# Layer 1 of a two-layer decoder trunk: attention's results and gates stored by token tiles, rows of dilation 16 by halves of the sequence

## The chip, the cores and the metric

The kernel runs on one core of a Trainium2 chip. The metric is the device time of one launch in microseconds (us), the median of several runs. A core has TensorE (PE; its weight loads are listed apart as PEld), VectorE (DVE), ScalarE (ACT), GpSimd (POOL) and SyncE (SP), each with an instruction queue of its own that is worked through in order, and 16 DMA engines that move data between the chip's memory (HBM) and the on-chip memory (SBUF). A DMA is issued by an engine's queue, here SP's (queue 1 in the profile) or GpSimd's (queue 0), and lands some microseconds later.

## The reference, cut to what matters

One inference step of a two-layer trunk, for a prompt of 2048 tokens and 32 sample tokens (8 sequences of 4). D_MODEL is 1024; a layer's width splits into 768 for the mixer and 256 for attention over 256 memory tokens.

```python
def mixer_layer(x, mem_k, mem_v, branch, w_in, w_out, ln_g, ln_b):
    proj = x @ w_in
    u, gate, mq, mgate = jnp.split(proj, IN_SPLITS, axis=-1)
    y, aux = branch(u)
    y = y.astype(x.dtype) * jax.nn.silu(gate)
    m = mem_attention(mq, mem_k, mem_v).astype(x.dtype) * jax.nn.silu(mgate)
    out = jnp.concatenate([y, m], axis=-1) @ w_out
    return layer_norm(DEEPNORM_ALPHA * x + out, ln_g, ln_b), aux
```

Layer 0's branch is a diagonal state-space mixer. Layer 1's is dilated causal attention in three groups of four heads: windows of 128, 512 and 2048 tokens with dilation 1, 4 and 16, all over one shared K and V that are projected from the residual stream after layer 0. The three groups' outputs are weighted by a softmax over the groups' log-sum-exps, and K and V are outputs too.

## The kernel before

Activations stand transposed, features on the 128 partitions and tokens along the free axis; a token tile has 128 tokens, so there are 16 for the prompt and one (number 16) for the sample's 32. An fp32 product is made of three reduced-precision ones: `split` (lines 123 and 124) makes a rounded high part on ScalarE (`ch`, `XH`, `wh`) and the remainder on VectorE (`cl`, `XL`, `wl`), and `mm3` (lines 128 to 130) issues the three matmuls.

Layer 1 is a list of projections (units) on TensorE, between which generators of side work (memory attention, `dilated`, `dil_sample`) issue their own matmuls at a set rate. Each unit ends in an evacuation that stores its result to HBM: `evac_streams` stores rows of q and k to `e_qT` and `e_kT` with the tokens ordered by residue of the dilation (for dilation 16, in 16 runs of 64 tokens a row and half sequence), `evac_gate` (lines 286 to 294) makes SiLU gates with ScalarE and VectorE and stores them to `e_gA` and `e_gB` from SP. Its tile `s` has three buffers.

`mem_attention` stores its result `ct` to `e_cm` (line 972), `dilated` stores `oT`, 128 features x 2048 tokens, to `e_oT` after every four quarters (line 1637, six such stores), and `dil_sample_end` stores the sample's to `e_cs`; these go by GpSimd's queue. `dilated` loads q and k rows into `raw` (lines 1551, 1552) and splits them: ScalarE makes `qh`, VectorE `ql` (line 1005).

The last part is `out_last`. For each of the 17 token tiles (order 0 to 7, 16, 8 to 15) `cat_dilated` loads attention's result into `ot` in two DMAs, 2 feature tiles from `e_cm` (line 1833) and 6 from `e_oT` (1834), the gate (1837) and the groups' weights `fb` (1842), all from SP. GpSimd multiplies `ot` by `fb` (1848), VectorE multiplies it by the gate (1849), ScalarE and VectorE split it into `ch` and `cl`, TensorE does 2 x 8 x 3 matmuls of 512 columns, and VectorE adds the residual `xres` (line 1963), takes statistics (1964) and normalises (1933, 1934); GpSimd issues the store of `y`. `ot`, `gate` and `fb` have four buffers, `xres` three, `ch` and `cl` two. The tile two ahead is multiplied and the next one split before a tile's matmuls, and a tile's loads are asked for five tiles ahead; a load starts when a buffer is free, that is, when the `cl` of the tile four before is done. `first1` makes the first two tiles already during the last gate projections, in the buffers of others (`v`, `wraw`).

The order on each engine is made by a scheduler from the recorded program. SP has one queue for all its loads and stores: an instruction that waits holds all that come behind it.

Of the kernel before, what the change touches and what calls it, by code (L numbers as in the profile page):

```python
# [9 lines left out]
F32 = mybir.dt.float32  # L10
# [3 lines left out]
OP = mybir.AluOpType  # L14
# [4 lines left out]
D = 1024  # L19
# [40 lines left out]
class Trunk:  # L60
# [223 lines left out]
    def evac_gate(self, dst, m):  # L284

        nc = self.nc

        def f(hf, off, n, p):
            s = self.ev.tile([128, 512], F32, name="s", bufs=3)
            nc.scalar.activation(s[:, :n], p[:, :n], AF.Tanh, scale=0.5)  # L290
            nc.vector.scalar_tensor_tensor(s[:, :n], s[:, :n], 1.0, p[:, :n], op0=OP.add, op1=OP.mult)  # L291
            self.recent = s[0:1, 0:1]
            nc.sync.dma_start(dst[hf][m * 128:m * 128 + 128, off:off + n], s[:, :n])
        return f

    def evac_copy(self, dst, m):
        nc = self.nc
# [590 lines left out]
    def mem_attention(self, l, d, side):  # L888
# [3 lines left out]
        with self.pool("ma", side=side) as p, self.pool("maps", space=PSUM, side=side) as psum:  # L892
# [60 lines left out]
            def st3(m):  # L953
                j, t = divmod(m, 2)
                ht, c0 = at(j)
                if t == 0:
                    O[j] = psum.tile([128, 512], F32, name="o", bufs=1)
                o, pt = O[j], PT.pop(m)
                for y in range(2):
                    for k in range(2):  # L960
                        for h in range(2):
                            c = (ht * 2 + h) * 64
                            mm(o[h * 64:h * 64 + 64, (t * 2 + y) * 128:(t * 2 + y) * 128 + 128], V[:, k, c:c + 64],  # L963
                               pt[:, y, h, k], start=k == 0, stop=k == 1)
                if t < 1:
                    return
                ct = p.tile([128, 512], F32, name="ct", bufs=2)
                if l == 0:
                    v.scalar_tensor_tensor(ct, o, 0.5, MG[j], op0=OP.mult, op1=OP.mult)
                else:  # L970
                    self.copy_out(ct, o)
                self.q2.dma_start(d["cm"][ht * 128:ht * 128 + 128, c0:c0 + 512], ct)

            load(0)
            load(1)
# [26 lines left out]
    def split_q(self, qh, ql, raw):  # L1002

        self.nc.scalar.activation(qh, raw, AF.Copy, scale=-0.125)
        self.nc.vector.scalar_tensor_tensor(ql, raw, -0.125, qh.bitcast(F32), op0=OP.mult, op1=OP.subtract)

    def scores(self, s, q, k, ts, ks=slice(None)):

# [8 lines left out]
    def mem_sample(self, l, p, psum, d):  # L1017
# [54 lines left out]
        for c in range(2):  # L1072
            pp = slice(c * 64, c * 64 + 64)
            for ht in range(2):
# [4 lines left out]
                                           op0=OP.mult, op1=OP.mult)  # L1079
                else:  # L1080
                    v.tensor_copy(view(ct[pp], ht * NS, dims), src)
        self.q2.dma_start(d["cm"][:, S:NT].rearrange("(m p) t -> p m t", p=128), ct)

    def softmax_rows(self, p, s, n, name):

# [287 lines left out]
    def layer1_units(self, d):  # L1373
# [3 lines left out]
        def evac_streams(dst, m, outs):  # L1377

            g = m // 2
            dil = DILS[g]  # L1380
            rows = {}

            def f(hf, off, n, p):
                if off == 0:
                    rows[hf] = self.ev.tile([128, HALF], F32, name="row", bufs=2)
                row = rows[hf]
                b = min(n, HALF - off) // 64
                s0 = off // 64
                src = p[:, :b * 64]
                if g == 0:  # L1390
                    out, src = view(row, s0, [[1, b], [16, 64]]), src.rearrange("p (b k) -> p b k", k=64)
                elif g == 1:
                    out = view(row, s0 // 4, [[1, b // 4], [256, 4], [4, 64]])
                    src = src.rearrange("p (a r k) -> p a r k", r=4, k=64)
                else:
                    out = row[:, off:off + b * 64]
                self.copy_out(out, src)
                self.recent = row[0:1, 0:1]
                if n > b * 64:
                    u = self.ev.tile([128, NS], F32, name="us", bufs=2)  # L1400
                    nc.vector.tensor_copy(u, p[:, b * 64:n])
                    nc.sync.dma_start(dst[m * 128:m * 128 + 128, S:NT], u)
                    if outs:
                        nc.sync.dma_start(o["ks"][m * 128:m * 128 + 128, :], u)
                if off + b * 64 < HALF:
                    return
                run = HALF // dil
                to = [[NT, 128], [S // dil, dil], [1, run]]
                nc.sync.dma_start(dview(dst, m * 128 * NT + hf * run, to), row.rearrange("p (r k) -> p r k", r=dil))
                if not outs:  # L1410
                    return
                r = slice(m % 2 * 128, m % 2 * 128 + 128)
                if g == 2:
                    nc.sync.dma_start(o["k2"][r, :, hf * 64:hf * 64 + 64], row.rearrange("p (r k) -> p r k", r=dil))
                elif hf:
                    nc.sync.dma_start(o[f"k{g}"][r], view(row, run - 128, [[run, dil], [1, 128]]))
            return f
# [103 lines left out]
    def dilated(self, p, psum, g, d):  # L1521
# [18 lines left out]
        def load(j):  # L1540

            hp, qd = divmod(j, 4)
            c = g * 2 + hp
            k0 = max(qd * 4 - 1, 0) if g == 0 else qd * 4
            n = (qd * 4 + 4 - k0) * 128
            if qd == 0:
                NB[hp] = p.tile([128, 2, 256], F32, name="NB", bufs=2)
                self.q2.dma_start(NB[hp], i["nbias"][2 * c:2 * c + 2].rearrange("h p u -> p h u"))
            raw = p.tile([128, 512 + W], F32, name="raw", bufs=3)
            rows = slice(c * 128, c * 128 + 128)  # L1550
            self.q2.dma_start(raw[:, 0:512], d["qT"][rows, qd * 512:qd * 512 + 512])
            self.q2.dma_start(raw[:, 512:512 + n], d["kT"][rows, k0 * 128:k0 * 128 + n])
            RAW[j] = raw

        def load_v(j):
# [4 lines left out]
            self.q2.dma_start(V[j][:, 0:n // 128], dview(d["V"], (g * 16 + k0) * 32768 + hp * 128,  # L1560
                                                         [[256, 128], [32768, n // 128], [1, 128]]))

        def prep(j, part):

            qd = j % 4
            k0 = max(qd * 4 - 1, 0) if g == 0 else qd * 4
            n = (qd * 4 + 4 - k0) * 128
            raw = RAW[j]
            if part == 0:
                q = [p.tile([128, 512], F32R, name=nm, bufs=2) for nm in ("qh", "ql")]  # L1570
                self.split_q(*q, raw[:, 0:512])
                QK[j] = q, k0
            else:
                k = [p.tile([128, W], F32R, name=nm, bufs=2) for nm in ("kh", "kl")]
                self.split(k[0][:, 0:n], k[1][:, 0:n], raw[:, 512:512 + n])
                QK[j] = QK[j][0], k, k0

        def st1(m):
# [29 lines left out]
        def st3(m):  # L1608
# [25 lines left out]
                src = o.rearrange("p (s f k) -> p s f k", s=4, f=2)  # L1634
                self.copy_out(view(oT[hp], qd * 256, [[64, 4], [HALF, 2], [1, 64]]), src)
            if qd == 3:
                self.q2.dma_start(d["oT"][c * 128:c * 128 + 128, :], oT[hp])

        load(0)
        load_v(0)  # L1640
# [158 lines left out]
    def dil_sample_end(self, p, psum, d):  # L1799
# [17 lines left out]
        for g in range(3):  # L1817
# [5 lines left out]
                    v.tensor_copy(view(ct[pp], (g * 2 + ht) * NS, [[1, 8], [8, 4]]),  # L1823
                                  view(tp[pp], ht * 64 + c, [[8, 8], [2, 4]]))
            yield
        self.q2.dma_start(d["cs"].rearrange("(m p) t -> p m t", p=128), ct)

    def cat_dilated(self, d, bufs=2):
        nc = self.nc

        def load(p, tt, ts, n):
            ot = p.tile([128, 8, 128], F32, name="ot", bufs=bufs)
            nc.sync.dma_start(ot[:, 6:8, :n], d["cm"][:, ts].rearrange("(k p) t -> p k t", p=128))
            nc.sync.dma_start(ot[:, 0:6, :n], (d["oT"][:, ts] if tt < 16 else d["cs"]).rearrange("(k p) t -> p k t", p=128))
            gt = p.tile([128, 8, 128], F32, name="gate", bufs=bufs)
            h, a = (0, tt * 128) if tt < 8 else (1, tt * 128 - HALF)
            nc.sync.dma_start(gt[:, :, :n], d["g"][h][:, a:a + n].rearrange("(k p) t -> p k t", p=128))
            fb = None
            if tt < 16:
                fb = p.tile([128, 6, 128], F32, name="fb", bufs=bufs)  # L1840
                for h in range(2):
                    nc.sync.dma_start(fb[h * 64:h * 64 + 64], dview(d["f"], (tt * 2 + h) * 768, [[0, 64], [128, 6], [1, 128]]))
            return ot, gt, fb
# [155 lines left out]
def _dram1(pool, d):  # L1999
    def t(name, *shape):  # L2000
        return pool.tile(list(shape), F32, name="e_" + name)

    return {"x1": d["x1"], "x1T": d["x1T"], "qT": t("qT", MIX, NT), "kT": t("kT", MIX, NT), "V": t("V", 3, 16, 128, 256),
            "vs": t("vs", NS, MIX), "g": (t("gA", D, HALF), t("gB", D, XW)), "mq": t("mq", MEMW, NT),
            "mk": d["mk"], "mv": d["mv"], "cm": t("cm", MEMW, NT), "cs": t("cs", MIX, NS), "oT": t("oT", MIX, S), "st": t("st", 3, 2, 4, S),
            "f": t("f", 16, 2, 6, 128)}


OUTS = {"y": (NT, D), "ssm_p": (128, G), "ssm_s": (128, 24, 2, 8), "mem_k": (2, 256, 256), "mem_v": (2, 256, 256),
        "k0": (256, 1, 128), "k1": (256, 4, 128), "k2": (256, 16, 128), "ks": (MIX, NS), "v0": (128, 256), "v1": (4, 128, 256),  # L2010
        "v2": (16, 128, 256), "vs": (NS, MIX), "n_cache_dil1_kv": (8, 124, 512), "n_cache_dil4_kv": (8, 508, 512),
        "n_cache_dil16_kv": (8, 2044, 512)}

# [161 lines left out]
```

## Time and profile before

| | us |
|---|---|
| median of 3 runs (lowest, highest) | 1985.59 (1984.99, 1986.73) |
| the profiled execution | 1987.37 |
| its span, first to last instruction | 1985.6 |
| TensorE busy in the span | 1933.8 (97 %) |
| VectorE busy | 1177.6 (59 %) |
| ScalarE busy | 687.6 (35 %) |
| GpSimd busy | 419.0 (21 %) |
| mean granted clock of TensorE | 0.991 |

All times of rows are counted from the span's start. An engine's idle time is put down to what ended last before the instruction started; a releaser is inferred from events, so two things that end together can be taken for each other. TensorE's matmuls are pipelined: a duration is longer than the distance from one start to the next. The granted clock is 1.00 at 2.4 GHz and 0.50 at 1.2 GHz.

### The profile page before, as it was taken

What the parts mean: (1) busy time and instruction counts of PE and PEld (TensorE: products, weight loads), DVE (VectorE), ACT (ScalarE), POOL (GpSimd) and SP (SyncE); (2) the same over time, 40 slices, a digit from 0 to 9 for tenths busy, and PEclk for the clock granted to TensorE, in tenths of its full rate; (3) what the DMA queues carried; (4) which work ended last, traced back from release to release, by engine and by line L of the source; (5) the groups of instructions that cost most, each with busy time, mean ns of one, the idle gap of its engine ahead of it and who ended that gap; (6) DMA issues with size and microseconds to landing.
All of it is one profiled execution on the core that took longest, in us unless ns stands there. A gap on an engine that the chain in (4) does not pass through costs nothing.

```text
span 1985.6 us, 35812 instructions
## 1 busy us (share of the span) xinstructions
PE 1933.8 (97%) x13446; PEld 1649.3 (83%) x13446; DVE 1177.6 (59%) x2758; ACT 687.6 (35%) x1585; POOL 419.0 (21%) x754
## 2 busy tenths in 40 slices
PE   8999999999989999999999999999999999999998
PEld 6789888888769988787898879898888877888777
DVE  8639989885575756667456336532651246345685
ACT  5333222333453421115445226522661246231110
POOL 0404444313332012220000020003102200412220
PEclk9999999999999999999999999999999999999999
DMA  7685556656367899978533266437648636759951
GB/s 227 173 252 133 163 170 188 203 184 219 111 170 220 238 307 347 362 268 262 165 124 115 90 222 195 135 91 200 192 119 247 223 111 191 256 169 263 285 164 70
DMA packets 410694, 388.44 MB, mean 196 GB/s; under 512 B 99801, under 2 KB 356233, under 8 KB 407241
## 3 DMA queue, kind: packets, MB, share of 16 engines
q1 hardware_dynamic: 384472, 257.52, 44.5%
q0 software_dynamic: 26048, 128.63, 19.0%
q8 instruction: 106, 1.74, 0.4%
q14 instruction: 68, 0.55, 0.1%
HBM read 280.30 MB, written 150.27 MB: 217 GB/s over the span
## 4 chain that ended last, share of the span: by engine, by line
PE 77%; DVE 9%; DMA 8%; issue 2%; POOL 2%; SPq 1%; ACT 1%; DVEq 0%; POOLq 0%; ACTq 0%
PE mm L128 20%; PE mm L129 20%; PE mm L130 20%; PE s L1014 4%; PE o L1620 2%; PE tp L1605 2%; DMA bcraw<-in_ssm_bc 2%; PE o L963 2%; DMA ot<-e_oT 2%; PE tp L950 1%; DMA xraw<-in_xT 1%; DVE wl L124 1%; DVE H L675 1%; PE tp L1366 1%; DMA craw<-d_cm 1%
## 5 line engine op out<-in xcount | busy, mean ns | idle before, releaser
L128 PE MATMUL mm<-XH,wh 128*128 128x512 f32 (+2 forms) x1520 | 546.9, 360 | 13.8 <-ACT wh L123 7.4
L129 PE MATMUL mm<-XH,wl 128*128 128x512 f32 (+2 forms) x1520 | 540.3, 356 | 0.3 <-DVE wl L124 0.3
L130 PE MATMUL mm<-XL,wh 128*128 128x512 f32 (+2 forms) x1520 | 538.2, 355 | 1.5 <-DVE XL L124 1.4
L128 PEld LDWEIGHTS mm<-XH,wh 128*128 128x128 f32 x1520 | 287.5, 189 | 60.8 <-ACT wh L123 8.0
L130 PEld LDWEIGHTS mm<-XL,wh 128*128 128x128 f32 x1520 | 287.3, 189 | 44.7 <-DVE XL L124 4.1
L129 PEld LDWEIGHTS mm<-XH,wl 128*128 128x128 f32 x1520 | 287.2, 189 | 41.3 <-issue 3.6
L129 PE MATMUL mm<-WOH,cl 128*128 128x512 f32 (+1 forms) x512 | 198.4, 387 | 4.8 <-DVE cl L124 4.8
L128 PE MATMUL mm<-WOH,ch 128*128 128x512 f32 (+1 forms) x512 | 199.6, 391 | 0.5 <-ACT ch L123 0.5
L130 PE MATMUL mm<-WOL,ch 128*128 128x512 f32 (+1 forms) x512 | 198.8, 388 | 0.0
L124 DVE TENSOR_TENSOR wl<-wraw,wh 128x1024 fp32r<-128x1024 f32 (+1 forms) x87 | 103.5, 1189 | 55.0 <-ACT wh L123 54.5
L124 DVE TENSOR_TENSOR XL<-xraw,XH 128x512 fp32r<-128x512 f32 (+2 forms) x176 | 98.7, 595 | 36.6 <-ACT XH L123 35.9
L129 PEld LDWEIGHTS mm<-WOH,cl 128*128 128x128 f32 x512 | 96.7, 189 | 26.6 <-DVE cl L124 6.1
L128 PE MATMUL mm<-v,XH 128*128 128x256 f32 (+1 forms) x408 | 118.0, 289 | 0.0
L129 PE MATMUL mm<-v,XL 128*128 128x256 f32 (+1 forms) x408 | 116.1, 285 | 0.0
L130 PE MATMUL mm<-v,XH 128*128 128x256 f32 (+1 forms) x408 | 115.4, 283 | 0.0
L130 PEld LDWEIGHTS mm<-WOL,ch 128*128 128x128 f32 x512 | 96.6, 189 | 21.3
L128 PEld LDWEIGHTS mm<-WOH,ch 128*128 128x128 f32 x512 | 96.6, 189 | 21.0 <-ACT ch L123 0.9
L123 ACT ACTIVATE XH<-xraw 128x512 fp32r<-128x512 f32 (+2 forms) x176 | 91.7, 554 | 53.8 <-DMA xraw<-in_xT 15.6
L1594 ACT ACTIVATE P<-P,st 128x128 f32<-128x128 f32 (+1 forms) x192 | 86.1, 451 | 50.4 <-DVE st L1592 50.2
L123 ACT ACTIVATE wh<-wraw 128x1024 fp32r<-128x1024 f32 (+1 forms) x87 | 89.3, 1027 | 23.6 <-DMA wraw<-in_w_in 10.2
L1592 DVE CUSTOM_DVE_ANT_0 P<-s,NB 128x128 f32<-128x128 f32 (+1 forms) x192 | 58.7, 362 | 60.3 <-PE s L1014 60.0
L291 DVE SCALAR_TENSOR_TENSOR s<-s,mm 128x512 f32<-128x512 f32 (+2 forms) x80 | 46.7, 583 | 75.0 <-ACT s L290 69.2
(407 smaller groups left out, 3662.4 us busy)
## 6 DMA issues: line engine op xcount, KB each, us to landing
out_n_cache_dil_kv<-in_cache_dil_kv POOLq DMA_DIRECT2D x64, 512.0 KB, 5.9
wraw<-in_w_in SPq DMA_DIRECT2D x63, 512.0 KB
xraw<-d_x1TA SPq DMA_DIRECT2D x48, 256.0 KB
wraw<-in_w_kv SPq DMA_DIRECT2D x24, 512.0 KB
xraw<-in_xT SPq DMA_DIRECT2D x40, 256.0 KB
kv<-in_c_kT POOLq DMA_DIRECT2D x18, 512.0 KB, 5.5
kv<-in_c_v POOLq DMA_DIRECT2D x18, 512.0 KB, 5.1
xres<-in_x SPq DMA_DIRECT2D x16, 512.0 KB
```

Source lines behind the costliest of these rows:

```text
L123: self.nc.scalar.activation(hi, src, AF.Copy)
L124: self.nc.vector.tensor_tensor(lo, src, hi.bitcast(F32), op=OP.subtract)
L128: mm(out, wh, xh, start=first, stop=False)
L129: mm(out, wl, xh, start=False, stop=False)
L130: mm(out, wh, xl, start=False, stop=last)
L291: nc.vector.scalar_tensor_tensor(s[:, :n], s[:, :n], 1.0, p[:, :n], op0=OP.add, op1=OP.mult)
L963: mm(o[h * 64:h * 64 + 64, (t * 2 + y) * 128:(t * 2 + y) * 128 + 128], V[:, k, c:c + 64], pt[:, y, h, k], start=k == 0, stop=k == 1)
L1014: self.nc.tensor.matmul(s[:, h], a[pp, ts], b[pp, ks], start=n == 0, stop=n == 3, tile_position=(h * 64, 0))
L1592: v.tensor_tensor_reduce(out=P[:, h, y, lo:], in0=s[:, h, y, lo:], in1=NB[hp][:, h, lo:], scale=1.0, scalar=3e38, op0=OP.add, op1=OP.min, ...
L1594: nc.scalar.activation(P[:, h, y, lo:], P[:, h, y, lo:], AF.Exp, scale=-1.0, bias=at(0, hh, T + y), accum_out=at(1, hh, T + y))
L1605: nc.tensor.transpose(tp[:, h, k], P[:, h, y, k * 128:k * 128 + 128], ident)
L1620: mm(o[h * 64:h * 64 + 64, (t * 2 + y) * 128:(t * 2 + y) * 128 + 128], V[j][:, T + y - 1 + k - k0, h * 64:h * 64 + 64], pt[:, y, h, k], st ...
```

## The change

Layer 1's gates and the joined results of both attentions get new arrays in HBM, `e_g` and `e_cat`, each [17 token tiles][128 partitions][8 feature tiles][128 tokens]. What one token tile needs is then 4 KB without a break for each partition: `ot` is one DMA and `gate` one. Their stores are cut into pieces of 512 B (128 tokens) by a new function `by_tiles`, with a DMA of its own for the sample's 32 columns. For dilation 16 the rows of q and k (and the output `k2`, which the host puts in order) are stored as they stand, by halves of the sequence; `dilated` then loads two runs of 1 KB a row and reorders in the views that the splits read, for which `split_q` takes two VectorE operations.

```diff
@@ evac_gate
-            nc.sync.dma_start(dst[hf][m * 128:m * 128 + 128, off:off + n], s[:, :n])
+            if isinstance(dst, tuple):
+                nc.sync.dma_start(dst[hf][m * 128:m * 128 + 128, off:off + n], s[:, :n])
+            else:
+                self.by_tiles(dst, m, hf * HALF + off, n, s)
...
+    def by_tiles(self, dst, m, a, n, s, q=None):
+        q = q or self.nc.sync
+        w = min(a + n, S) - a
+        if w:
+            q.dma_start(dview(dst, a * D + m * 128, [[1024, 128], [131072, w // 128], [1, 128]]),
+                        s[:, :w].rearrange("p (t k) -> p t k", k=128))
+        if n > w:
+            q.dma_start(dview(dst, S * D + m * 128, [[1024, 128], [1, NS]]), s[:, w:n])
@@ mem_attention (l is the layer)
-                self.q2.dma_start(d["cm"][ht * 128:ht * 128 + 128, c0:c0 + 512], ct)
+                if l == 0:
+                    self.q2.dma_start(d["cm"][ht * 128:ht * 128 + 128, c0:c0 + 512], ct)
+                else:
+                    self.by_tiles(d["cat"], 6 + ht, c0, 512, ct, self.q2)
@@ split_q
-        self.nc.vector.scalar_tensor_tensor(ql, raw, -0.125, qh.bitcast(F32), op0=OP.mult, op1=OP.subtract)
+        parts = [(ql, raw, qh)]
+        if len(raw.shape) == 4:
+            parts = [[x[:, :, f] for x in parts[0]] for f in range(2)]
+        for lo, x, hi in parts:
+            self.nc.vector.scalar_tensor_tensor(lo, x, -0.125, hi.bitcast(F32), op0=OP.mult, op1=OP.subtract)
@@ evac_streams
-                to = [[NT, 128], [S // dil, dil], [1, run]]
-                nc.sync.dma_start(dview(dst, m * 128 * NT + hf * run, to), row.rearrange("p (r k) -> p r k", r=dil))
+                if g == 2:
+                    nc.sync.dma_start(dst[m * 128:m * 128 + 128, hf * HALF:hf * HALF + HALF], row)
+                else:
...
-                    nc.sync.dma_start(o["k2"][r, :, hf * 64:hf * 64 + 64], row.rearrange("p (r k) -> p r k", r=dil))
+                    nc.sync.dma_start(o["k2"][r, hf], row)
@@ dilated
-            self.q2.dma_start(raw[:, 0:512], d["qT"][rows, qd * 512:qd * 512 + 512])
-            self.q2.dma_start(raw[:, 512:512 + n], d["kT"][rows, k0 * 128:k0 * 128 + n])
+            for src, b, w, c0 in (("qT", 0, 512, qd * 512), ("kT", 512, n, k0 * 128)):
+                if g < 2:
+                    self.q2.dma_start(raw[:, b:b + w], d[src][rows, c0:c0 + w])
+                else:
+                    self.q2.dma_start(raw[:, b:b + w].rearrange("p (f k) -> p f k", f=2),
+                                      dview(d[src], c * 128 * NT + qd * 256, [[NT, 128], [HALF, 2], [1, 256]]))
...
-                self.q2.dma_start(d["oT"][c * 128:c * 128 + 128, :], oT[hp])
+                self.by_tiles(d["cat"], c, 0, S, oT[hp], self.q2)
@@ dil_sample_end
-        self.q2.dma_start(d["cs"].rearrange("(m p) t -> p m t", p=128), ct)
+        self.q2.dma_start(dview(d["cat"], S * D, [[1024, 128], [128, 6], [1, NS]]), ct)
@@ cat_dilated
-            nc.sync.dma_start(ot[:, 6:8, :n], d["cm"][:, ts].rearrange("(k p) t -> p k t", p=128))
-            nc.sync.dma_start(ot[:, 0:6, :n], (d["oT"][:, ts] if tt < 16 else d["cs"]).rearrange("(k p) t -> p k t", p=128))
+            nc.sync.dma_start(ot[:, :, :n], d["cat"][tt, :, :, :n])
             gt = p.tile([128, 8, 128], F32, name="gate", bufs=bufs)
-            h, a = (0, tt * 128) if tt < 8 else (1, tt * 128 - HALF)
-            nc.sync.dma_start(gt[:, :, :n], d["g"][h][:, a:a + n].rearrange("(k p) t -> p k t", p=128))
+            nc.sync.dma_start(gt[:, :, :n], d["g"][tt, :, :, :n])
```

SP's queue has 711 rows for 719 before (a row stands for like instructions in a run). Near the end of `out_last`, where the loads of the last tiles are issued, SP had two DMAs for each `ot`:

```order
L1842 DMA fb<-e_f 64x768 x2
L1837 DMA gate<-e_gB 128x8x128
L1889 DMA xres<-d_x_96 128x1024
L1833 DMA ot<-e_cm 128x2x128
L1834 DMA ot<-e_oT 128x6x128
L1833 DMA ot<-e_cm 128x2x128
L1834 DMA ot<-e_oT 128x6x128
L1889 DMA xres<-d_x_96 128x1024 x2
```

The same place on SP with the change (`e_cat` holds attention's results, `e_g` the gates):

```order
L1877 DMA fb<-e_f 64x768 x2
L1872 DMA gate<-e_g 128x1024
L1924 DMA xres<-d_x_96 128x1024
L1870 DMA ot<-e_cat 128x1024 x2
L1924 DMA xres<-d_x_96 128x1024 x2
```

The sequence is the same, with one `ot` load for two. During the last gate projections, where SP loads what `first1` needs (into `v` and `ot`) between stores of gates and loads of weights, SP had before:

```order
L199 DMA wraw<-in_w_in 128x8x128
L293 DMA e_gB<-s 128x256
L1834 DMA v<-e_oT 128x6x128
L1834 DMA ot<-e_oT 128x6x128
L293 DMA e_gB<-s 128x512
L293 DMA e_gB<-s 128x288
L199 DMA wraw<-in_w_in 128x8x128
```

With the change, on SP at that place:

```order
L199 DMA wraw<-in_w_in 128x8x128
L304 DMA e_g<-s 128x2x128
L1870 DMA v<-e_cat 128x1024
L1872 DMA v<-e_g 128x1024
L1870 DMA ot<-e_cat 128x1024
L304 DMA e_g<-s 128x4x128
L304 DMA e_g<-s 128x2x128
L307 DMA e_g<-s 128x32
L199 DMA wraw<-in_w_in 128x8x128
```

The loads of `e_cm` that stood far ahead of this place are now part of the loads of `e_cat`, a gate load (`v<-e_g`) stands between them, and the store of 288 columns has become one of two tiles and one of the sample's 32 columns. On TensorE the 11982 matmuls of the program are the same in number and kind; on VectorE the order around lines 1849 and 124 of `out_last` is the same.

## Rows read from the trace of the kernel before

**Rows 1.** Page, part 1: busy us (share of the span) and instructions.
```profile
PE 1933.8 (97%) x13446; PEld 1649.3 (83%) x13446; DVE 1177.6 (59%) x2758; ACT 687.6 (35%) x1585; POOL 419.0 (21%) x754
```
**Rows 2.** Waits of TensorE, 960 to 1986: total us, times, longest.
```profile
PE mm L129 <- DVE cl L124: 3.8, 1, 3.8
PE tp L1605 <- ACT P L1594: 0.4, 1, 0.4
```
**Rows 3.** Stretches around the wait: length, busy us by engine, clock, DMA share, GB/s.
```profile
1900.00:1904.00 4.00, 4.00 (x19) 3.22 (x18) 3.90 (x6) 1.24 (x2) 1.19 (x1) 1.00 0.00 0
1904.00:1908.40 4.40, 0.69 (x3) 0.20 (x2) 4.37 (x7) 0.00 (x0) 0.55 (x1) 0.80 0.28 68
1908.40:1913.40 5.00, 4.93 (x12) 3.87 (x13) 4.07 (x7) 1.24 (x2) 0.38 (x1) 0.50 0.57 176
1913.40:1920.00 6.60, 6.60 (x30) 5.32 (x29) 5.04 (x7) 0.30 (x1) 1.99 (x2) 0.99 0.48 165
```
**Rows 4.** Timeline of VectorE: start, us, line, operation [idle before <- releaser].
```profile
1893.63 0.68 DVE L1957 BATCH_NORM_STATS2 st<-r 32x6 f32<-32x512 f32 x1
1898.26 1.23 DVE L1849 SCALAR_TENSOR_TENSOR ot<-ot,gate 128x1024 f32<-128x1024 f32 x1 [3.94 <-POOL ot L1848]
...
1907.20 1.21 DVE L124 TENSOR_TENSOR cl<-ot,ch 128x1024 fp32r<-128x1024 f32 x1
```
**Rows 5.** Timeline of GpSimd.
```profile
1896.38 1.84 POOL L1848 TENSOR_TENSOR ot<-ot,fb 128x768 f32<-128x768 f32 x1 [3.52 <-DMA ot<-e_oT]
```
**Rows 6.** Chain of waits, 1885 to 1986: start, us, what.
```profile
1893.63 4.60 DMA xres<-d_x
```
**Rows 7.** Timeline of SP's queue: start and us of the issue.
```profile
1886.71 0.46 SPq L1837 DMA_DIRECT2D gate<-e_gB  x1
...
1888.44 0.36 SPq L1833 DMA_DIRECT2D ot<-e_cm  x1
1888.86 1.16 SPq L1834 DMA_DIRECT2D ot<-e_oT  x1
1890.10 1.56 SPq L1833 DMA_DIRECT2D ot<-e_cm  x1
```
**Rows 8.** Stretch in which the critical `ot` tile is loaded, columns as in rows 3.
```profile
1889.00:1896.30 7.30, 7.30 (x33) 5.88 (x32) 5.12 (x10) 0.29 (x1) 0.58 (x1) 1.00 1.00 314
```
**Rows 9.** Waits, 1860 to 1910.
```profile
DVE ot L1849 <- POOL ot L1848: 14.6, 4, 4.1
POOL ot L1848 <- DMA ot<-e_oT: 12.1, 3, 6.3
```
**Rows 10.** DMA queues, 1894 to 1896: packets, MB, share of 16 engines.
```profile
q1 hardware_dynamic: 827, 0.41, 69.7%
q0 software_dynamic: 55, 0.23, 27.5%
```
**Rows 11.** Stretch of the last gate projections, columns as in rows 3.
```profile
1660.00:1740.00 80.00, 79.48 (x662) 66.38 (x660) 36.83 (x111) 30.15 (x82) 21.29 (x34) 1.00 0.79 250
```
**Rows 12.** Line 1637, the `oT` store: issue ns min/median/max, first and last start; landing.
```profile
L1637 POOL DMA_DIRECT2D e_oT<-oT x6: 558/571/603, 1270.5 to 1692.7; - x6
...
DMA to landing us min/median/max: 4.2/4.9/6.8
```
**Rows 13.** Line 1560, the load of V in 512 B pieces, likewise.
```profile
L1560 POOL DMA_DIRECT2D V<-e_V x24: 749/757/897, 1174.5 to 1668.0; - x24
...
DMA to landing us min/median/max: 3.2/3.8/8.7
```
**Rows 14.** Timeline of SP's queue behind the last `oT` store.
```profile
1697.70 0.37 SPq L1834 DMA_DIRECT2D v<-e_oT  x1
1698.12 5.49 SPq L1834 DMA_DIRECT2D ot<-e_oT  x1
```
**Rows 15.** VectorE by line and shape, 1160 to 1700: busy us, mean ns | idle before.
```profile
L1005 DVE SCALAR_TENSOR_TENSOR ql<-raw,qh 128x512 fp32r<-128x512 f32 x24 | 16.4, 685 | 4.4 <-ACT qh L1004 4.4
```
**Rows 16.** Line 1849: ns min/median/max; the shortest has 256 columns.
```profile
L1849 DVE SCALAR_TENSOR_TENSOR ot<-ot,gate x16: 406/1225/1228, 1752.2 to 1924.9; 128x1024 f32<-128x1024 f32 x15, 128x256 f32<-128x256 f32 x1
```

More of the change, by code (lines that the diff above doesn't have):

```diff
@@ L1081, in mem_sample @@
                     v.tensor_copy(view(ct[pp], ht * NS, dims), src)
-        self.q2.dma_start(d["cm"][:, S:NT].rearrange("(m p) t -> p m t", p=128), ct)
+        if l == 0:
+            self.q2.dma_start(d["cm"][:, S:NT].rearrange("(m p) t -> p m t", p=128), ct)
+        else:
+            self.q2.dma_start(dview(d["cat"], S * D + 768, [[1024, 128], [128, 2], [1, NS]]), ct)
     def softmax_rows(self, p, s, n, name):
@@ L1407, in f @@
                 run = HALF // dil
-                to = [[NT, 128], [S // dil, dil], [1, run]]
-                nc.sync.dma_start(dview(dst, m * 128 * NT + hf * run, to), row.rearrange("p (r k) -> p r k", r=dil))
+                if g == 2:
+                    nc.sync.dma_start(dst[m * 128:m * 128 + 128, hf * HALF:hf * HALF + HALF], row)
+                else:
+                    to = [[NT, 128], [S // dil, dil], [1, run]]
+                    nc.sync.dma_start(dview(dst, m * 128 * NT + hf * run, to), row.rearrange("p (r k) -> p r k", r=dil))
                 if not outs:
@@ L1550, in load @@
             rows = slice(c * 128, c * 128 + 128)
-            self.q2.dma_start(raw[:, 0:512], d["qT"][rows, qd * 512:qd * 512 + 512])
-            self.q2.dma_start(raw[:, 512:512 + n], d["kT"][rows, k0 * 128:k0 * 128 + n])
+            for src, b, w, c0 in (("qT", 0, 512, qd * 512), ("kT", 512, n, k0 * 128)):
+                if g < 2:
+                    self.q2.dma_start(raw[:, b:b + w], d[src][rows, c0:c0 + w])
+                else:
+                    self.q2.dma_start(raw[:, b:b + w].rearrange("p (f k) -> p f k", f=2),
+                                      dview(d[src], c * 128 * NT + qd * 256, [[NT, 128], [HALF, 2], [1, 256]]))
             RAW[j] = raw
@@ L1561, in load_v, with order @@
                                                          [[256, 128], [32768, n // 128], [1, 128]]))
+        def order(x, stored=False):
+            if g < 2:
+                return x
+            return x.rearrange("p (f r k) -> p r f k" if stored else "p (r f k) -> p r f k", f=2, k=64)
         def prep(j, part):
@@ L1570, in prep @@
                 q = [p.tile([128, 512], F32R, name=nm, bufs=2) for nm in ("qh", "ql")]
-                self.split_q(*q, raw[:, 0:512])
+                self.split_q(*(order(x) for x in q), order(raw[:, 0:512], True))
                 QK[j] = q, k0
@@ L1574, in prep @@
                 k = [p.tile([128, W], F32R, name=nm, bufs=2) for nm in ("kh", "kl")]
-                self.split(k[0][:, 0:n], k[1][:, 0:n], raw[:, 512:512 + n])
+                self.split(order(k[0][:, 0:n]), order(k[1][:, 0:n]), order(raw[:, 512:512 + n], True))
                 QK[j] = QK[j][0], k, k0
@@ L2003, in _dram1 @@
     return {"x1": d["x1"], "x1T": d["x1T"], "qT": t("qT", MIX, NT), "kT": t("kT", MIX, NT), "V": t("V", 3, 16, 128, 256),
-            "vs": t("vs", NS, MIX), "g": (t("gA", D, HALF), t("gB", D, XW)), "mq": t("mq", MEMW, NT),
-            "mk": d["mk"], "mv": d["mv"], "cm": t("cm", MEMW, NT), "cs": t("cs", MIX, NS), "oT": t("oT", MIX, S), "st": t("st", 3, 2, 4, S),
+            "vs": t("vs", NS, MIX), "g": t("g", 17, 128, 8, 128), "mq": t("mq", MEMW, NT),
+            "mk": d["mk"], "mv": d["mv"], "cat": t("cat", 17, 128, 8, 128), "st": t("st", 3, 2, 4, S),
             "f": t("f", 16, 2, 6, 128)}
 OUTS = {"y": (NT, D), "ssm_p": (128, G), "ssm_s": (128, 24, 2, 8), "mem_k": (2, 256, 256), "mem_v": (2, 256, 256),
-        "k0": (256, 1, 128), "k1": (256, 4, 128), "k2": (256, 16, 128), "ks": (MIX, NS), "v0": (128, 256), "v1": (4, 128, 256),
+        "k0": (256, 1, 128), "k1": (256, 4, 128), "k2": (256, 2, HALF), "ks": (MIX, NS), "v0": (128, 256), "v1": (4, 128, 256),
         "v2": (16, 128, 256), "vs": (NS, MIX), "n_cache_dil1_kv": (8, 124, 512), "n_cache_dil4_kv": (8, 508, 512),
@@ L2166 @@
     for g, (name, win) in enumerate((("cache_dil1_kv", 128), ("cache_dil4_kv", 512), ("cache_dil16_kv", 2048))):
-        k = o[f"k{g}"].transpose(2, 1, 0).reshape(win, 256)
+        k = o[f"k{g}"]
+        if g == 2:
+            k = k.reshape(256, 2, 16, 64).transpose(0, 2, 1, 3).reshape(256, 16, 128)
+        k = k.transpose(2, 1, 0).reshape(win, 256)
         v = o[f"v{g}"]
```

## The prediction, made before the changed kernel was run

> **What bounds the kernel now.** I read the busy shares first: TensorE works 97 % of the span [rows 1], so time can be won only where it idles or runs slowly. The list of TensorE's waits over layer 1 (960 to 1986 us) has two entries: 3.8 us on `cl` of line 124 and 0.4 us on `P` [rows 2]. The table by stretches puts the first at 1904 to 1908.4, where TensorE is busy 0.69 of 4.40 us, and shows a second price behind it: from 1908.4 to 1913.4 the granted clock is 0.50, the 1.2 GHz level, and 12 matmuls fill 4.93 us, 0.41 each; in the next stretch, at 0.99, 30 matmuls fill 6.60 us, 0.22 each [rows 3]. That is 12 x 0.19 = 2.3 us more. So 3.8 + 2.3 = 6.1 us is all that a perfect `out_last` could give back; everywhere else in layer 1 TensorE runs on.
>
> Why was `cl` late? VectorE works in order. In its timeline it stood ready at 1893.63 + 0.68 = 1894.3, then idled 3.94 us before `ot*gate` (line 1849), which began at 1898.26; from there it is busy without a break (3.90 of 4.00 us, then 4.37 of 4.40 [rows 3]) up to the `cl` that starts at 1907.20 and ends at 1908.4, where TensorE resumes [rows 4]. GpSimd's timeline says why 1849 was late: `ot*fb` (line 1848) waited for a transfer, ran from 1896.38 for 1.84 us and ended at 1898.22 [rows 5]. The chain of waits names another cause for the same moment, the xres load, 4.60 us from 1893.63 to 1898.23 [rows 6]; but xres is no operand of 1849, it only landed together with GpSimd's end. SP's timeline shows the two loads of that `ot` tile issued at 1888.44 and 1888.86 [rows 7]; with GpSimd starting at 1896.38, the tile took 7.9 us. The 16 DMA engines were full meanwhile: share 1.00 from 1889 to 1896.3 [rows 8]. It was no single accident: from 1860 to 1910 VectorE waited for line 1848 four times, 14.6 us in all, and 1848 itself 12.1 us for `ot` loads [rows 9].
>
> **What a piece costs.** In 1894 to 1896 queue 1 carried almost only 512 B pieces (827 packets, 0.41 MB) and queue 0 4 KB ones (55, 0.23 MB) [rows 10]. 69.7 % of 16 engines x 2 us is 22.3 us, 27 ns a packet; 27.5 % is 8.8 us, 160 ns a packet. A 512 KB tile is therefore 1024 x 27 / 16 = 1.73 us of all engines in 512 B pieces, 128 x 160 / 16 = 1.28 us in 4 KB rows: 0.45 us saved by each `ot` load and each gate load. The page "DMA: Bandwidth & Descriptors" of the Trainium skill (Specifications) asks for 512 B or more for line rate; by that rule 512 B pieces already run at it and the loads would gain nothing. The row disagrees, 19 against 26 bytes per ns. The same page (Why small descriptors are slow) gives 3 bus cycles over 16 for 512 B, which by estimate is 16 % and not 35 % more per byte than in long rows; the saving would be half of mine.
>
> **The change part by part.**
> Loads of `out_last`. Two `ot` loads become one of 128 rows, the gate load has 128 rows instead of 1024 pieces. In front of the critical landing stand one gate load and two tiles of `ot` [rows 7], so the transfers alone shrink by 3 x 0.45 = 1.35 us: the lower bound. The upper one is a load of just this shape in just this place: xres, 512 KB in 4 KB rows, 4.60 us [rows 6]; 1888.44 + 4.60 = 1893.0, 3.3 us before GpSimd's 1896.38. I take the upper one, since it is the same form through the same full engines, and since the three waits before it in [rows 9] shrink too and bring VectorE to its place earlier, which I don't count. GpSimd then runs 1893.1 to 1894.9, VectorE idles 0.6 instead of 3.94, and its later work, which needs no result of TensorE younger than one tile (11 us), moves up by 3.3. TensorE's wait falls from 3.8 to 0.5 us. Whether the clock still falls after 0.5 us is not shown for this stage; the 0.4 us wait at 1680 [rows 2] left a granted clock of 1.00 in 1660 to 1740 [rows 11]. I take it as kept, 2.3 us.
> Stores of attention's results. Each of six `oT` stores turns from 128 rows of 8 KB into 2048 pieces of 512 B on GpSimd's queue. Landing was 4.2 / 4.9 / 6.8 us [rows 12]. The nearest row with 512 B pieces on that queue is the V load, a quarter of the bytes: 3.2 / 3.8 / 8.7 us [rows 13]. Bounds: no change, or four V loads end to end, 15.2 us by the median, 35 us by the longest. I take 2048 x 27 / 16 = 3.5 us of transfer against 256 x 160 / 16 = 2.6 us, one microsecond more. Only the last store has somebody near behind it: SP issues `v<-oT` at 1697.70, 5 us after the store at 1692.7, then was held by the next issue for 5.49 us until 1703.6 [rows 14], and TensorE lost nothing [rows 2]. That 5.49 us issue of 768 pieces becomes one of 128 rows. Cost 0 while the store lands before about 1702.
> Gate stores. A 512-column store has 512 pieces for 128 rows of 2 KB; 512 x 27 / 16 = 0.86 us of transfer. By 160 ns for 4 KB, the old form is at least 0.64 us. The 0.2 us each, and eight more small stores on SP for the sample's columns, lie beside projections in which TensorE had no wait [rows 2]. If that cover were gone, ScalarE's `s` buffers would come free later by the same 0.2 us; I count 0, at most 1.
> Rows of dilation 16. 12 stores lose 2048 pieces of 256 B for 128 rows of 4 KB, cheaper, hidden as before. `split_q` has two 128x256 operations for one of 128x512 in eight places: 0.685 us each now [rows 15], at most 2 x 0.41 [rows 16], so 8 x 0.13 = 1.1 us of VectorE in attention, hidden behind the same uninterrupted TensorE; 1.1 us if not. GpSimd's issues of three-dimensional patterns take 757 ns instead of 571 by the medians [rows 12, 13], 0.2 us more each, on an engine that is busy 21 of 80 us in 1660 to 1740 [rows 11].
> Sum: -3.3 - 2.3 = -5.6 us. The profiled execution took 1987.37 us (span 1985.6), 1.8 above the median of 1985.59; I take the difference off the median: 1980.0 us.
>
> **The rivals.** A change under 0.2 % (4.0 us) can't be told from none here.
> 1. Half a rescue. Only the transfers shorten: 1.35 us, or some 2 us with SP's shorter issues; TensorE still waits about 2 us and the clock still drops. 1983.6 to 1984.2 us. For it: VectorE has no gap from 1900 to 1908.4 [rows 3], so each microsecond must come from the landing. Against: xres's 4.60 us in the same congestion.
> 2. Nothing. The pieces don't matter, or the `fb` tiles (unchanged, also operands of line 1848) land last in `ot`'s place; GpSimd starts where it did, 1985.6 us. The rule of 512 B above would give this. Against: [rows 9] name `ot` for all 12.1 us, and 27 ns a piece [rows 10].
> 3. Slower. The last `oT` store holds SP, which issues in order: behind `v<-e_cat` stand two more loads, three gate stores and the weights of the next projection (the second place of the order shown). It decides from a landing past 1702, 9.3 us after the issue. With four V medians, 15.2 us, it lands at 1707.9: 5.9 us that TensorE waits, and the clock's 2.3 us once more; less the 5.6 us won, 1988.2 us. For it: 16 times as many pieces on a queue that software feeds, and V's longest 8.7. Against: V's 512 B pieces land as soon as other loads of that queue.
>
> **How the numbers follow.** Forecast 0.52 (own range 1978.6 to 1981.6: the full 6.1 us, and the spread of the runs, 0.9, on one side; 4 us on the other). Half a rescue 0.20, nothing 0.14, slower 0.14. All of the forecast counts as faster, with a little of rival 1: 0.55. Rivals 1 and 2, without that and without what unseen small costs would push over the bound, 0.30. Slower 0.15. The range goes from 1978.0 to 1987.0: it takes in rivals 1 and 2 and leaves out most of 3.
>
> **What would show it.** Right: no wait of TensorE on `cl` above 0.6 us, no stretch at half clock after 1900, `ot` landing in 4 to 5 us, the DMA share between 1889 and 1896 clearly under 1.00, VectorE's waits for line 1848 well below 14.6 us. Wrong: the wait on `cl` stands at 2 us or more (rivals 1 and 2: look whether `ot` or `fb` lands last), or a new wait of TensorE near 1700 to 1710 with SP held at `v<-e_cat` (rival 3). A new wait in attention on `ql` would show the split operations uncovered.

## The result and the profile after

The changed kernel took 1975.42 us (median; 1973.91 to 1981.53), its ratio to the kernel before 0.9938, 95 % interval [0.9918, 0.9957]. The forecast was 1980.0 us, range 1978.0 to 1987.0, with the sum -5.6 us. The middle of the ratio is -12.3 us, so the side was right, the size less than half of what came, and the median lies 2.6 us below the stated range. The kernel before scatters more than its first three runs showed: the eight executions that the ratio rests on have a median of 1990.45 us (1984.99 to 2001.09), not the 1985.59 from which the forecast was counted. Beside the first experiments 35 executions of it went from 1983.09 to 2001.05 us, while the six of the changed kernel in its second run went from 1977.87 to 1981.08.

The profiled execution of the changed kernel has a span of 1973.8 us, against 1985.6. Page, part 1, answering to [rows 1], and the first row of its part 3 (packets, MB, share of 16 engines):

```profile
PE 1926.5 (98%) x13446; PEld 1643.7 (83%) x13446; DVE 1178.9 (60%) x2766; ACT 686.9 (35%) x1585; POOL 425.9 (22%) x754
...
q1 hardware_dynamic: 344904, 257.52, 43.7%
```

The bytes of SP's queue are the same, in 39,568 fewer packets. Waits of TensorE in layer 1, as in [rows 2]:

```profile
PE mm L129 <- DVE cl L124: 0.9, 1, 0.9
PE o L1829 <- DMA kv<-in_c_v: 0.3, 1, 0.3
```

The 0.9 us do not lie at the old place but at 1801, near the start of `out_last`. At the old place, where the program of TensorE now stands some 5 us earlier, it runs on, and at full clock. Stretches of the profile after, columns as in [rows 3]; the first is the load stretch of [rows 8]:

```profile
1878.40:1886.00 7.60, 7.60 (x34) 6.13 (x33) 7.40 (x13) 0.29 (x1) 0.58 (x1) 1.00 0.83 310
1890.00:1894.00 4.00, 4.00 (x18) 3.21 (x18) 3.93 (x6) 1.25 (x2) 0.00 (x0) 1.00 0.00 0
1894.00:1900.00 6.00, 6.00 (x27) 4.62 (x26) 5.90 (x9) 0.50 (x2) 0.55 (x1) 1.00 0.31 87
1900.00:1904.00 4.00, 4.00 (x19) 3.22 (x18) 3.44 (x5) 0.75 (x1) 0.57 (x1) 1.00 0.55 169
```

Timelines of VectorE, GpSimd and SP after, answering to [rows 4, 5, 7]:

```profile
1885.38 0.68 DVE L1992 BATCH_NORM_STATS2 st<-r 32x6 f32<-32x512 f32 x1
1888.21 2.86 DVE L1884 SCALAR_TENSOR_TENSOR ot<-ot,gate 128x1024 f32<-128x1024 f32 x1 [2.14 <-POOL ot L1883]
...
1898.14 1.21 DVE L124 TENSOR_TENSOR cl<-ot,ch 128x1024 fp32r<-128x1024 f32 x1
```

```profile
1886.34 3.64 POOL L1883 TENSOR_TENSOR ot<-ot,fb 128x768 f32<-128x768 f32 x2 [1.73 <-DMA ot<-e_cat]
```

```profile
1880.20 0.80 SPq L1870 DMA_DIRECT2D ot<-e_cat  x2
```

The same chain stands there, with smaller numbers: `ot` issued at 1880.20, GpSimd starting at 1886.34 (6.1 us, before 7.9), VectorE idle for 2.14 us instead of 3.94, and `cl` done at 1899.35. TensorE's timeline says that this was just in time (start, us):

```profile
1899.17 0.40 PE L128 MATMUL mm<-WOH,ch 128*128 128x512 f32 x1
1899.40 0.50 PE L129 MATMUL mm<-WOH,cl 128*128 128x512 f32 x1
```

Waits from 1855 to 1905, the stretch of [rows 9] moved by those 5 us:

```profile
DVE ot L1884 <- POOL ot L1883: 11.4, 4, 3.2
...
POOL ot L1883 <- DMA fb<-e_f: 6.3, 1, 6.3
...
POOL ot L1883 <- DMA ot<-e_cat: 5.1, 3, 1.8
```

GpSimd waits 5.1 us for `ot` instead of 12.1; part of it has passed to `fb`. Cutting two traces of the kernel before (the second is the first experiment's) and three of the changed kernel at the starts of the same matmuls shows where the time went, in us:

| stretch of TensorE's program | before | changed |
|---|---|---|
| up to the first `mm<-v,XH`, early in layer 1 | 1014.5, 1011.7 | 1010.1, 1014.6, 1012.2 |
| from there to `out_last` | 770.6, 773.1 | 768.6, 768.5, 768.8 |
| `out_last` to the last matmul | 192.6, 194.4 | 187.6, 188.4, 186.3 |
| behind the last matmul | 7.9, 7.9 | 7.4, 7.4, 7.4 |

The first stretch, which no edit touches, scatters by 4.5 us and tells nothing; the 4.4 us that it was shorter in the first pair are chance. `out_last` lost 6.1 us between the means, layer 1 ahead of it 3.2, the end 0.5.

### The profile page after: what moved, and what is told of

The parts are those of the page before. It is cut to its first block, busy times and chain, and to the rows that moved or that the text cites. A ratio compares the mean times of both kernels' runs of the same rounds, so it can differ in the third digit from the quotient of the medians.

```text
span 1973.8 us, 35795 instructions
## 1 busy us (share of the span) xinstructions
PE 1926.5 (98%) x13446; PEld 1643.7 (83%) x13446; DVE 1178.9 (60%) x2766; ACT 686.9 (35%) x1585; POOL 425.9 (22%) x754
## 4 chain that ended last, share of the span: by engine, by line
PE 83%; DMA 7%; DVE 5%; issue 1%; SPq 1%; ACT 1%; POOL 1%; DVEq 0%; ACTq 0%; POOLq 0%
PE mm L128 22%; PE mm L129 22%; PE mm L130 22%; PE s L1034 4%; PE o L1657 2%; PE tp L1642 2%; PE o L976 2%; PE tp L963 1%; DMA wraw<-in_w_in 1%; DMA bcraw<-in_ssm_bc 1%; DMA kv<-in_c_v 1%; PE tp L1389 1%; DVE wl L124 1%; DMA craw<-d_cm 1%; PE v L627 1%
## 5 line engine op out<-in xcount | busy, mean ns | idle before, releaser
L128 PE MATMUL mm<-XH,wh 128*128 128x512 f32 (+2 forms) x1520 | 546.7, 360 | 12.3 <-ACT wh L123 7.9
```

What stands on the lines that cost most here:

```text
L128: mm(out, wh, xh, start=first, stop=False)
```

## The experiments

The experiments ran in three groups of four kernels (the expectations say call for group), each group on one chip with the kernel before beside it, and all ratios below are to that. The waits are TensorE's on `cl` in layer 1.

| kernel | ratio, 95 % interval | median us | waits on `cl`: sum, times, longest | `out_last` |
|---|---|---|---|---|
| before again (group 1) | 0.9997 [0.9978, 1.0016] | 1990.32 | 5.6, 1, 5.6 | 194.4 |
| rows of dilation 16 only (1) | 1.0009 [0.9994, 1.0024] | 1992.08 | 7.4, 2, 6.3 | 197.6 |
| new arrays, 512 B pieces (1) | 0.9983 [0.9966, 1.0000] | 1987.26 | 4.5, 1, 4.5 | 192.5 |
| tiles without the rows (1) | 0.9956 [0.9938, 0.9975] | 1983.19 | none | 186.3 |
| gates only (2) | 0.9971 [0.9954, 0.9987] | 1988.37 | 4.2, 2, 3.2 | 192.5 |
| joined results only (2) | 0.9963 [0.9947, 0.9979] | 1986.68 | 4.5, 2, 4.0 | 192.9 |
| changed kernel (2) | 0.9922 [0.9900, 0.9944] | 1978.63 | 1.6, 2, 1.0 | 188.4 |
| changed, `fb` and xres earlier (2) | 0.9923 [0.9903, 0.9944] | 1979.99 | 1.6, 1, 1.6 | 188.3 |
| changed kernel (3) | 0.9931 [0.9913, 0.9949] | 1978.38 | none | 186.3 |
| changed, first xres earlier (3) | 0.9935 [0.9915, 0.9955] | 1977.40 | none | 186.4 |
| tiles without the rows (3) | 0.9947 [0.9930, 0.9964] | 1981.31 | none | 186.3 |
| changed, one load more (3) | 0.9939 [0.9920, 0.9958] | 1979.56 | 7.2, 3, 5.0 | 196.0 |

**The kernel before, again.** No edit.

Expected:

> The kernel before, once more. Theory (the wait on cl in out_last is built into its order of loads): ratio 1.000 within 0.002, and its second profile shows again a wait of TensorE on cl of 3 to 4 us around 1900 with a stretch of half clock behind it. Rival (the wait was a chance of one execution): the wait is under 1 us in this profile. Besides: the part of layer 0 (first 960 us), which no edit touches and which came out 4.3 us shorter in the profile after, should move by the same few us from one execution of the kernel before to the other, if those 4.3 us are chance.

The wait is no chance. Its second trace has it with 5.6 us, and the half clock behind it; TensorE's waits, and the stretches around the wait:

```profile
PE mm L129 <- DVE cl L124: 5.6, 1, 5.6
```

```profile
1904.10:1909.90 5.80, 0.36 (x2) 0.01 (x1) 5.73 (x7) 0.00 (x0) 0.55 (x1) 0.82 0.21 37
1909.90:1914.60 4.70, 4.50 (x11) 3.54 (x12) 4.19 (x7) 1.24 (x2) 0.12 (x1) 0.50 0.64 205
1914.60:1920.00 5.40, 5.40 (x25) 4.34 (x24) 3.60 (x5) 0.00 (x0) 2.26 (x2) 1.00 0.38 127
```

So the ceiling of 6.1 us in the prediction was one execution's: here it would have been 5.6 + 11 x 0.19 = 7.7 us. The untouched first stretch moved by 2.8 us between the two traces.

**Tiles without the rows.** `evac_streams`, the loads of `dilated` and `split_q` as before, the rest as in the change:

```diff
-                if g == 2:
-                    nc.sync.dma_start(dst[m * 128:m * 128 + 128, hf * HALF:hf * HALF + HALF], row)
```

Expected:

> The change without the rows of dilation 16: only attention's results and gates by token tiles. Theory (the loads of out_last are the gain): the whole gain, 5 to 12 us under the kernel before, no wait on cl above 1 us near the end. Rival (rows of dilation 16 carry a part, since attention came out 1.9 us shorter): 2 us or more short of the changed kernel's gain.

-8.8 us, and no wait on `cl` at all, as the theory had it. It is also 3.5 us short of the changed kernel's 12.3, the sign of the rival, but the two were not measured side by side.

Run again beside the changed kernel. Expected:

> The change without the rows of dilation 16, once more, now on the same chip as the changed kernel. Theory (the rows' part wins some 2 us in layer 1's attention and projections, as in every profile so far that has it): 1 to 4 us slower than the changed kernel of this call. Rival (a difference of chips): the same within 1 us.

1981.31 against 1978.38 us, 2.9 us slower in the medians (1978.59 to 1983.42 against 1976.18 to 1979.41; the intervals of the ratios overlap), as the theory had it. The stretch ahead of `out_last` took 768.3 to 769.1 us in the seven traces with tiles and rows, 770.3 to 773.1 in the six without rows; without TensorE's listed waits in it, 768.3 to 768.5 and 769.4 to 771.8. So waits don't explain these 1 to 3.5 us; differently ordered side work on TensorE, by a few instructions, is all that the traces show. Their cause stays open.

**Rows of dilation 16 only.** The counterpart: the kernel before with that part of the change.

```diff
+                if g == 2:
+                    nc.sync.dma_start(dst[m * 128:m * 128 + 128, hf * HALF:hf * HALF + HALF], row)
```

Expected:

> Only the rows of dilation 16 by halves (stores of 4 KB rows, loads of two runs of 1 KB, split_q in two operations); results and gates stored as before. Theory: within 2 us of the kernel before, the wait on cl of 3 to 4 us and the half clock still there. Rival (the rows' part helps attention): 2 us or more faster, with the wait on cl unchanged.

Not faster, as the theory had it: +1.8 us, the interval holding no change. Its `out_last` has the largest wait of all, 6.3 us, and one of 3.0 us on a load of cached values came in the stretch ahead (772.8 us):

```profile
PE mm L129 <- DVE cl L124: 7.4, 2, 6.3
PE o L1810 <- DMA kv<-in_c_v: 3.0, 1, 3.0
```

Without that 3.0 us the stretch would be 769.8 us, among those without rows: what the rows win beside the tiles, they don't win alone, and why is not known. It doesn't hang on the waits of `out_last`, for the next kernel has rows, such a wait, and 769.1 us.

**New arrays, 512 B pieces.** `e_cat` and `e_g` feature tile by feature tile, one DMA per load, but of 1024 pieces:

```diff
-            nc.sync.dma_start(ot[:, :, :n], d["cat"][tt, :, :, :n])
+            nc.sync.dma_start(ot[:, :, :n], dview(d["cat"], tt * 131072, [[128, 128], [16384, 8], [1, n]]))
```

Expected:

> The changed kernel with the same arrays laid out feature tile by feature tile, so that each load of ot and gate is still one DMA but reads 1024 pieces of 512 B; stores have the same pieces as in the change. Theory (the pieces of the loads set the landing): the ot load takes 7 us or more in the full stretch, TensorE waits on cl for 2 us or more, the time lies within 2 us of the kernel before. Rival (one DMA in place of two and SP's shorter issues are the gain): as fast as the changed kernel, wait under 1 us.

The wait is back with 4.5 us, `out_last` takes 192.5 us as before, and of the gain 3.4 us are left, a little more than the 2 us that the theory allowed. So in `out_last` the length of the pieces in the loads is what counts; one DMA in place of two wins nothing there that the trace shows. But the theory's landing failed: the critical `ot` tile took 6.6 us, not 7 or more. SP and GpSimd:

```profile
1883.78 1.59 SPq L1870 DMA_DIRECT2D ot<-e_cat  x2
```

```profile
1890.42 3.65 POOL L1883 TENSOR_TENSOR ot<-ot,fb 128x768 f32<-128x768 f32 x2 [2.23 <-DMA ot<-e_cat]
```

The tile was asked for late; the table under "The landing" below takes this up. The page "DMA: Bandwidth & Descriptors" of the Trainium skill (Specifications) takes 512 B as enough for line rate; these runs disagree, 0.9983 against 0.9922 to 0.9938 for long rows. This kernel has all the new stores too, and TensorE has no listed wait on them.

**Joined results only, gates only.** Each layout alone, without the rows; the other one as before:

```diff
+            nc.sync.dma_start(ot[:, :, :n], d["cat"][tt, :, :, :n])
```

```diff
+            nc.sync.dma_start(gt[:, :, :n], d["g"][tt, :, :, :n])
```

Expected:

> Of the change only attention's joined results by token tiles: ot in one DMA of 4 KB rows; gates, and rows of dilation 16, as before. Theory (ot's landing is what GpSimd waits for): half or more of the gain of both, 4 to 8 us, wait on cl under 2 us. Rival (all pieces in the queue count alike, gates as much as ot): about half, and a wait of 2 to 3 us with the half clock left.

Expected:

> Of the change only the gates by token tiles: 4 KB rows in the gate loads, 512 B pieces and eight more stores on SP in the gate stores; ot in two DMAs of 512 B pieces as before. Theory: a quarter of the gain or less, 0 to 3 us, wait on cl of 2 us or more still there. Rival (all pieces count alike): 3 to 6 us.

-7.4 and -5.8 us by the ratios, with waits left in both traces:

```profile
PE mm L129 <- DVE cl L124: 4.5, 2, 4.0
```

```profile
PE mm L129 <- DVE cl L124: 4.2, 2, 3.2
```

The first fence is `ot`'s, the second the gates'. For the gates the rival was right: long rows in a load for which GpSimd doesn't wait help nearly as much as in `ot`, within the intervals. For the joined results the time lies in the theory's range, and the longest wait, 4.0 us, above both. That the two share the DMA engines in the full stretch of [rows 8], so that shorter transfers of either bring the other forward, is the likely reason, but these traces don't show it: `out_last` takes 192.9 and 192.5 us in them, as before, and the traced executions, 1988.95 and 1989.12 us, were among the slower of their twelve. The sum of both gains, 13.2 us, is more than the 8.8 and 10.6 us of both together, though not clearly so within the intervals.

**One load more.** The changed kernel, and the gate tile's 512 KB read again in 4 KB rows:

```diff
+                more = p.tile([128, 8, 128], F32, name="more", bufs=2)
+                nc.sync.dma_start(more, d["g"][tt])
```

Expected:

> The changed kernel with one more load per prompt tile in out_last: the same 512 KB of gates once more, in 4 KB rows, into a tile that nobody reads. All loads stay in long rows; only the DMA engines' work for a tile goes up by 1.28 us by the price of 160 ns for 4 KB, to about what 512 B pieces cost for ot and gate. Theory (what counts is the work in the shared DMA queue, whoever's it is): a wait on cl of 2 to 5 us and half a clock come back, 3 to 8 us slower than the changed kernel. Rival (what counts is that ot and gate themselves come in long rows): within 2 us of the changed kernel.

In the trace the theory holds. The DMA share is full again and the wait back, with a lowered clock behind it, and GpSimd's row shows the late start (`more`, which the view names, is no operand of it):

```profile
PE mm L129 <- DVE cl L124: 7.2, 3, 5.0
```

```profile
1897.00:1902.00 5.00, 5.00 (x23) 4.04 (x22) 2.48 (x4) 0.00 (x0) 0.55 (x1) 1.00 1.02 281
1902.40:1907.70 5.30, 0.28 (x2) 0.00 (x0) 2.98 (x4) 0.00 (x0) 1.80 (x1) 0.97 1.04 284
1907.70:1912.70 5.00, 4.97 (x15) 3.98 (x16) 4.93 (x6) 1.24 (x2) 2.45 (x2) 0.69 1.02 288
```

```profile
1902.89 1.80 POOL L1886 TENSOR_TENSOR ot<-ot,fb 128x768 f32<-128x768 f32 x1 [3.75 <-DMA more<-e_g]
```

The times don't follow it: 1979.56 us against 1978.38, not 3 to 8 us more. The profiled execution, 1985.44 us, was the slowest of six, the others lie from 1975.05 to 1980.08. So added work in the queue can bring the wait back, and in most executions it seems not to; by the times the rival was right. As evidence for the shared queue this run is inconclusive; what speaks for it is the time of the gates alone.

**Two orders of loads.** In the changed kernel GpSimd waits long for `fb`, and the wait at 1801 stands behind the first xres. First `fb` ahead of the gate and xres ahead of tile 2's loads, then the latter alone:

```diff
-            load(2)
             load_x(0)
+            load(2)
             load_x(1)
```

Expected:

> The changed kernel with each tile's fb loads issued ahead of its gate load (GpSimd needs ot and fb, VectorE needs the gate only after GpSimd), and the first xres load ahead of the loads of tile 2. Theory (in the profile after GpSimd waited 45.5 us for fb in seven waits, and the one wait of 0.9 us left near 1801 stands behind the first xres): GpSimd's waits for fb fall by a third or more, the wait near 1801 goes, 0 to 1.5 us faster than the changed kernel. Rival (the scheduler, which orders VectorE anew from it, moves cl to a worse place): a new wait on cl, as fast or slower.

Expected:

> The changed kernel with only the first xres load put ahead of the loads of tile 2. Theory (the wait of about 1 us near 1801 to 1806, seen in both profiles of the changed kernel, stands behind the landing of that xres): this wait goes and no other comes, 1 to 1.5 us faster. Rival (VectorE's order is made anew from it, and the cl of tile 2 or a later one comes late instead): as fast or slower.

The first moved the wait instead of removing it (1.6 us, now at 1850) and cut GpSimd's waits for `fb` from 1778 to 1910 only from 44.4 to 40.8 us: as fast as the changed kernel. The second left TensorE without any listed wait in layer 1, and is not measurably faster either, 0.9935 against 0.9931 beside it; the changed kernel's own trace in the same group had no wait at 1801 either. Neither order measurably beats the changed kernel.

**The changed kernel, twice more.** No edit. Expected of its second run:

> The changed kernel once more, beside the others of this call. Theory: 0.990 to 0.996 of the kernel before, no wait of TensorE on cl above 1 us near 1890 to 1900 and no stretch at half clock behind it. Rival (the 12 us of the first comparison were partly a chance of two chips): 0.997 or more. Against the same change without the rows of dilation 16, which took 0.9956: up to 2 us less, if what attention won in the profile after is real, no difference if it is not.

Expected of its third, the measure of the third group:

> The changed kernel a third time, as the measure for the others of this call: 0.992 to 0.995 of the kernel before, no wait on cl above 1.1 us.

Both held, 0.9922 and 0.9931: the gain of the first comparison is no chance of two chips.

## Why the prediction was right, and where its sizes were wrong

- **Place and chain: right.** The wait on `cl` goes, the half clock with it, and 512 B pieces bring them back. The DMA share in the load stretch fell from 1.00 to 0.83, as foretold; VectorE's waits for GpSimd only from 14.6 to 11.4 us, not well below. The sign "no wait of TensorE on `cl` above 0.6 us" failed by a wait at another place, 0.9 and 1.0 us near 1801 to 1807 in two of three traces.
- **The landing: mis-sized, and not the main thing.** The step "1888.44 + 4.60 = 1893.0", a load like xres's, gave 3.3 us, and an `ot` landing in 4 to 5 us. Measured were 6.1 instead of 7.9, so 1.8, near the lower bound of 1.35. What closed the gap is the part that the prediction named and left uncounted, the tiles before: VectorE stood ready at 1886.06, and at the same place of TensorE's program would have before at 1894.31 - 5.1 = 1889.2, so 3.1 us earlier. Together 4.9, less 1.0 because a longer line 1849 and its successors took it back: 3.9 us, all of the old wait. Of the 3.1, some 1.1 are only that TensorE came to the place later, through its wait at 1801. The other traces confirm that the tiles before count most. SP may ask for this `ot` tile when the `cl` of an earlier tile has freed its buffer; SP's waits from 1880 to 1892 in the first trace of the kernel before:

```profile
SPq L1833 <- DVE cl L124: 0.6, 1, 0.6
```

The times of this load in the traces, in us, counted from the start of `out_last`:

| kernel | `ot` asked for | from there to GpSimd's start | TensorE's wait there |
|---|---|---|---|
| tiles without the rows, two traces | 95.9, 96.0 | 7.1, 7.8 | none |
| changed kernel, three traces | 101.4, 101.9, 99.6 | 6.1, 6.5, 6.7 | none, 0.6, none |
| before, two traces | 103.4, 104.5 | 7.9, 7.7 | 3.8, 5.6 |
| joined results only | 103.4 | 8.0 | 4.0 |
| gates only | 104.1 | 7.0 | 3.2 |
| new arrays, 512 B pieces | 104.5 | 6.6 | 4.5 |
| rows of dilation 16 only | 108.2 | 8.0 | 6.3 |

The wait goes with an early request, not with a short landing: tiles without the rows land it in up to 7.8 us and don't wait, 512 B pieces in 6.6 and do. That the shorter loads of the tiles before make the request early fits the order of releases; no run tests it by itself.
- **The price of a piece: near.** The 4 KB packets of [rows 10] were not loads but the store of `y` on GpSimd's queue. SP's own queue, in the load stretch before (1889 to 1896.3) and after (1878.4 to 1886):

```profile
q1 hardware_dynamic: 3033, 1.97, 89.6%
```

```profile
q1 hardware_dynamic: 682, 2.33, 81.7%
```

By bytes over the engines' busy time that is 19 and 23 bytes per ns, some packets of other sizes among them; the prediction had 19 and 26.
- **The clock: right.** 2.3 us in the first trace; a wait of 0.6 us at the same place, in its second run, left it at 1.00 in the changed kernel, as assumed for 0.5.
- **The ceiling: wrong.** "6.1 us is all that a perfect `out_last` could give back" was read from one execution, whose wait of 3.8 us was the smaller of two. For that execution it was near: `out_last` took 192.6 us in it, 186.3 where nothing waits. And "everywhere else in layer 1 TensorE runs on" set the rows of dilation 16 to nothing; beside the tiles, though not alone, they won about 2 us there, without a wait that the list of waits would have shown. Over the traces the account is 6.1 + 3.2 + 0.5 = 9.8 us.
- **The rest is open.** The ratios give 12.3, 15.5 and 13.7 us, 2.5 to 5.7 more than the traces. Part of it is which executions were traced: for the kernel before, 1987.37 and 1988.85 us, below its medians of 1990.45 to 1991.80; for the changed one, 1975.58, 1980.76 and 1976.53 us, around its medians of 1975.42 to 1978.63. What the slower executions of the kernel before lose can't be told without their traces. A clock lost outside the traces is not shown: over all executions of the second group the mean granted clock is 0.9937 for the changed kernel and 0.9912 for the one before, 0.0025 apart, and in the traces it already differs by more, 0.994 to 0.996 against 0.991 and 0.992.
- **Stores: cheap, dearer than thought.** An `oT` store lands in 7.1 us instead of 4.9 (one more was forecast), and its issue takes 1.18 us instead of 0.57 (0.76 was forecast). Line 304 with `oT`, answering to [rows 12], and SP behind the last store, answering to [rows 14]:

```profile
L304 POOL DMA_DIRECT2D e_cat<-oT x6: 1167/1177/1204, 1266.0 to 1685.2; - x6
...
DMA to landing us min/median/max: 6.1/7.1/8.1
```

```profile
1693.21 0.33 SPq L1870 DMA_DIRECT2D v<-e_cat  x1
1693.63 0.39 SPq L1872 DMA_DIRECT2D v<-e_g  x1
1694.25 0.32 SPq L1870 DMA_DIRECT2D ot<-e_cat  x1
```

- **Rival 3: not entered.** SP was held until 8.0 us after the store's issue (1693.21 - 1685.2), 1.3 short of the 9.3 us from which it was to decide, and the 5.49 us issue behind it has become 0.32. TensorE is busy 80.00 of 80.00 us there:

```profile
1660.00:1740.00 80.00, 80.00 (x668) 68.12 (x665) 36.07 (x96) 28.10 (x73) 24.67 (x37) 1.00 0.75 235
```

- **`split_q`: right.** Two operations of 0.42 us for one of 0.685, and TensorE has no wait on `ql`.

## What to carry to other kernels

When the DMA engines are full in a stretch, look at every load in it, not only at the one that is waited for: longer rows in the gates alone were worth 5.8 us by the times. In a chain of prefetched tiles a shortened load can pay twice, once in its own landing and once through the tiles before it, whose buffers come free earlier; here the second was the larger. And a wait read from a single trace is one draw: trace the unchanged kernel twice before taking it for the ceiling.

## What the runs showed of the hardware

A store of 1 MB on GpSimd's queue in 2048 pieces of 512 B cost GpSimd 1.18 us to issue, twice the 0.57 us of 128 rows of 8 KB, and 2.2 us more to land. The part of the program that no edit touched scattered from 1010.1 to 1016.2 us over the traces of all kernels, more than many of the effects studied here.
